# Weights split into high and low parts once and kept in DRAM for the later row groups

## The chip, the cores and the metric

The kernel runs on one core of a Trainium2 chip. The metric is device time in microseconds (us) of one execution, the median of several runs; smaller is better.

## What is computed

One layer of a streaming encoder: 2048 prompt rows and 128 sample rows (8 batches of 16) of width 1024 are normalised, projected to 3072 columns, run through three kinds of attention with gates, projected back to 1024, normalised and added to the input. Cut to what matters here:

```
qa, ka, va, ga, qb, kb, vb, gb, qm, gm = split(rmsnorm(x, g_pre) @ w_in)
oa = band attention of 6 heads (own 64-row chunk and 8 before it, learned bias)
ob = grouped-query window attention of 6 heads (own chunk and 2 before it, ALiBi, sinks)
om = cross-attention of 4 heads into 256 memory tokens
y  = x + rmsnorm(concat(oa*silu(ga), ob*silu(gb), om*silu(gm)) @ w_out, g_post)
```

Everything is float32 and has to come out with nearly that accuracy. Both projections use the same weights for all rows.

## The kernel before

**Precision.** A projection is three passes of matmuls in a reduced-precision type (fp32r): high part times high part, high times low, low times high. So each operand exists as a pair: a rounded high part and the low part that is left over. `project_T` (line 184) multiplies a 128-column weight tile with 512 rows in 24 matmuls (8 blocks of the inner dimension by three passes); `project_N` (line 196) uses two weight tiles for one block of 128 rows, again 24 matmuls.

**Weights.** w_in and w_out lie in DRAM as a list of 128 x 1024 tiles of 512 KB (`wt`; `W_TILES`, line 32). `load_w` (line 131) makes a pair of one: SP (SyncE, which issues most transfers) loads the tile into one of three `wraw` buffers (line 138), ACT copies it rounded into the high half of a `whl` buffer (line 139), and DVE or POOL in turn subtracts the two into the low half (line 140). `whl`, 1 MB each, has three buffers as well. `weights(name)` calls `load_w` at each use, so a tile is loaded and split again in each row group. Four more tiles (`wm`) are for the memory tokens, and one, "last", serves the end of the program alone.

**Rows.** The 2048 rows go in four groups of 512, groups 0 to 3; group 0 takes the 128 sample rows along. Each group projects (24 tiles), attends, and then projects out (8 tiles, "o", in the loop from line 907; in the last group in another form, with two tiles loaded into free parts of the arrays `xn` and `sh`, line 928). Steps of a group stand in a string of `ORDERS` (line 42): M is attention into memory, V, K, Pa and Pb project, Aa and Ab attend, S are the sample rows, X loads keys and values of the group before from DRAM, F finishes the group before (normalise, add x, store), L and N load and scale the next group's rows, Q projects some of the next group's columns.

**Who orders.** The program is written in that order, and a scheduler puts the instructions of each engine in a fixed sequence; an engine then takes its own strictly in order and waits for semaphores. SP is such a queue too: a transfer that waits for its buffer holds up all that stand behind it.

**Names for later.** `psT` and `psN` are the results of the two projections. In attention `sa` are scores, `sba` probabilities (lines 727 to 732: add bias and take the minimum on DVE, exponential on ACT, reciprocal and scaling on DVE), `pt` their transposes, which lines 208 and 209 split on ACT and DVE into `sh`; `oa`, `ob`, `om` (line 260) are the products with the values, merged by lines 267 and 268 into `sums`. `sbm` (line 653) and `sbb` (line 809) are the same for the memory and the window attention. Line 220 copies halves of q, line 891 splits the attention's result for the output projection on POOL.

Of the kernel before, what the change touches and what calls it, by code (L numbers as in the profile page):

```python
# [9 lines left out]
F32 = mybir.dt.float32  # L10
F32R = mybir.dt.float32r
# [20 lines left out]
W_TILES = [("q", 6), ("g", 6), ("q", 7), ("g", 7), ("v", 0, 0), ("v", 0, 1),  # L32
           ("k", 0), ("q", 0), ("g", 0), ("k", 1), ("q", 1), ("g", 1), ("v", 1, 0), ("v", 1, 1),
           ("k", 3), ("q", 3), ("g", 3), ("q", 4), ("g", 4), ("q", 5), ("g", 5), ("k", 2), ("q", 2), ("g", 2)]
W_TILES += [("o", c, r) for c in range(4) for r in range(2)] + [("last",)]

LAST, EARLY = 2, 2
# [8 lines left out]
W_AT = {name: i for i, name in enumerate(W_TILES)}  # L46
# [3 lines left out]
def encoder_step(ctx, tc, x_p, x_s, xT0, xT, mem, memT, wt, wm, g_pre, g_mem, g_post, rel_rev, sink,  # L50
# [3 lines left out]
    pe, act, dve, pool, sp = nc.tensor, nc.scalar, nc.vector, nc.gpsimd, nc.sync  # L54

    cst = ctx.enter_context(tc.tile_pool(name="cst", bufs=1))
    wrawp = ctx.enter_context(tc.tile_pool(name="wrawp", bufs=3))
    whlp = ctx.enter_context(tc.tile_pool(name="whlp", bufs=3))
    xp = ctx.enter_context(tc.tile_pool(name="xp", bufs=2))
    nbp = ctx.enter_context(tc.tile_pool(name="nbp", bufs=2))  # L60
    sbp = ctx.enter_context(tc.tile_pool(name="sbp", bufs=5))
# [7 lines left out]
    drp = ctx.enter_context(tc.tile_pool(name="drp", bufs=1, space=DRAM))  # L69
# [54 lines left out]

    skew_d = drp.tile([6, 128 * 768], F32, name="skew_d")
    e_d = drp.tile([6, 768], F32, name="e_d")
    kctx_d = [drp.tile([128, 2, 512], F32, name=f"kctx{i}") for i in range(6)]
    vctx_d = [drp.tile([128, 4, 256], F32, name=f"vctx{i}") for i in range(6)]


    def load_w(src, hl=None):

        raw = wrawp.tile([128, 1024], F32, tag="wraw", name="wraw")
        if hl is None:
            hl = whlp.tile([128, 2, 1024], F32R, tag="whl", name="whl")
        eng = (dve, pool)[turn["s"] % 2 if turn["s"] > 2 else 0]
        for m in [slice(0, 1024)] if turn["s"] else [slice(0, 512), slice(512, 1024)]:
            sp.dma_start(out=raw[:, m], in_=src[:, m])
            act.activation(hl[:, 0, m], raw[:, m], AF.Copy)  # L139
            eng.tensor_tensor(hl[:, 1, m], raw[:, m], hl[:, 0, m].bitcast(F32), ALU.subtract)  # L140
        turn["s"] += 1
        return hl

    def weights(*name):
        return load_w(wt[W_AT[name]])

    def rms_scale(ss, n, rstd):
        dve.tensor_scalar(rstd[:, :n], ss[:, :n], 1.0 / D, EPS, ALU.mult, ALU.add)
# [338 lines left out]
    def gains():  # L487
        t = xp.tile([128, D], F32, tag="x", name="gpost")
        sp.dma_start(out=t, in_=g_post.partition_broadcast(128))
        return t, stp.tile([128, 32], F32, tag="pst", name="pst", bufs=2)  # L490
# [96 lines left out]
    for g in range(NG):  # L587
# [262 lines left out]
        for step in ORDERS[g].split():  # L850
            what, j = step[:-1], int(step[-1])
# [41 lines left out]
        if g < NG - 1:  # L893
# [13 lines left out]
            for c in range(4):  # L907
                ws = [weights("o", c, r) for r in range(2)]
# [11 lines left out]
        for c in range(EARLY):  # L920
            ws = [weights("o", c, r) for r in range(2)]
# [3 lines left out]
                    act.activation(spare[:, i] if f == LAST else mo[:, i, f], ps[:, 128 * (f % 2):128 * (f % 2) + 128], AF.Copy)  # L925
        room = [t.rearrange("p (a b) -> p a b", a=2) for t in (sh[:, 5376:7424], xn[:, 8192:])]
        wl = weights("last")
        ws = [load_w(wt[W_AT["o", EARLY + j // 2, j % 2]], (room + [None] * 2)[j]) for j in range(4)]
        gpost, st = gains()
        for i in range(4):  # L930
            split_mixed(mixlast, i, LAST, mo[:, i, LAST])
# [2 lines left out]
            o = mo[:, i].rearrange("p a b -> p (a b)")  # L934
# [152 lines left out]
```

## Time and profile before

| | us |
|---|---|
| median of 3 runs (1195.86 to 1201.51) | 1199.81 |
| the profiled execution | 1199.29 |
| its span, first to last instruction | 1197.5 |

Row groups by the profile: group 0's output projection ends at about 414 us, group 1's at about 684 and group 2's at about 955; the first step of the next group (V) follows at once on PE, to about 429, 697 and 967. The profile lists for each engine its busy time, for each group of equal instructions their count, mean duration and the idle time ahead of them with what ended it, and for any stretch of time the busy time of each engine, the granted clock of TensorE (1.00 is full speed), and the busy share and rate of the 16 DMA engines. PE is TensorE's matmuls, PEld its loads of stationary operands, DVE, ACT and POOL are VectorE, ScalarE and GpSimd.

Matmuls are pipelined, and their busy time runs into each other; so a PE that is 100% busy in a stretch is issuing without a pause, and what it can lose shows as idle time or as a lower clock.

### The profile page before, as it was taken

How to read it: one execution, taken by the hardware profiler on the slowest of the kernel's cores; microseconds unless marked ns; L12 is line 12 of the kernel's file. 1: busy time of each engine (PE TensorE's matmuls, PEld its weight loads, DVE VectorE, ACT ScalarE, POOL GpSimd, SP SyncE). 2: the span in 40 equal slices, each digit the busy share in tenths (PEclk: the TensorE clock that was granted, in tenths of full speed). 3: DMA queues.
4: the chain of work that ended last, by engine and by line, in shares of the span. 5: the costliest groups of instructions: out<-in, count | busy, mean ns of one | idle time of the engine just before them, and what ended most of it. 6: DMA issues, size and time to landing. Idle time of an engine off the chain costs nothing.

```text
span 1197.5 us, 20992 instructions
## 1 busy us (share of the span) xinstructions
PE 1137.5 (95%) x7794; PEld 1024.5 (86%) x7794; DVE 840.0 (70%) x1911; ACT 689.5 (58%) x1609; POOL 362.2 (30%) x286
## 2 busy tenths in 40 slices
PE   7899999999989999999999999999988998999897
PEld 6789898897679988898888988898778987988797
DVE  7648666777784457779997336679997336679965
ACT  6546565655544565558664455557765444667652
POOL 5411210211261552122433552122333450221441
PEclk9899999999889999999999999999999998999999
DMA  7673552624621593333311493333321471432213
GB/s 264 211 226 130 172 181 57 232 83 151 240 71 53 176 341 119 110 111 112 126 58 36 133 360 115 111 114 123 115 63 36 129 285 54 126 97 89 90 54 106
DMA packets 62239, 163.43 MB, mean 136 GB/s; under 512 B 8109, under 2 KB 19379, under 8 KB 62137
## 3 DMA queue, kind: packets, MB, share of 16 engines
q1 hardware_dynamic: 58392, 152.66, 38.4%
q0 software_dynamic: 3744, 9.44, 2.7%
q8 instruction: 61, 1.00, 0.3%
q14 instruction: 42, 0.34, 0.1%
HBM read 140.95 MB, written 23.48 MB: 137 GB/s over the span
## 4 chain that ended last, share of the span: by engine, by line
PE 74%; DVE 16%; ACT 3%; issue 3%; DMA 2%; POOL 1%; SPq 0%; DVEq 0%; POOLq 0%; ACTq 0%
PE psT L191 33%; PE psN L202 23%; PE pt L247 5%; PE oa L260 4%; PE sa L241 3%; DVE sh L209 3%; DVE whl L140 1%; DVE sba L727 1%; PE om L260 1%; DVE sbb L798 1%; DVE sbb L809 1%; PE ss L358 1%; PE so L392 1%; PE ob L260 1%; PE sm L241 1%
## 5 line engine op out<-in xcount | busy, mean ns | idle before, releaser
L191 PE MATMUL psT<-xn,whl 128*128 128x512 f32 (+2 forms) x2400 | 531.8, 370 | 11.3 <-ACT whl L139 6.8
L191 PEld LDWEIGHTS psT<-xn,whl 128*128 128x128 f32 x2400 | 410.1, 192 | 73.9 <-ACT whl L139 7.1
L140 POOL TENSOR_TENSOR whl<-wraw,whl 128x1024 fp32r<-128x1024 f32 x64 | 155.7, 2433 | 357.5 <-ACT whl L139 303.7
L202 PE MATMUL psN<-whl,sh 128*128 128x256 f32 x1296 | 162.2, 283 | 1.5 <-POOL sh L891 1.3
L202 PEld LDWEIGHTS psN<-whl,sh 128*128 128x128 f32 x1296 | 156.4, 189 | 3.7 <-POOL sh L891 1.5
L139 ACT ACTIVATE whl<-wraw 128x1024 fp32r<-128x1024 f32 (+1 forms) x132 | 138.2, 1047 | 33.8 <-PE psN L202 13.7
L202 PE MATMUL psN<-whl,xn 128*128 128x256 f32 x1080 | 143.0, 283 | 3.1 <-ACT stgN L618 1.1
L202 PEld LDWEIGHTS psN<-whl,xn 128*128 128x128 f32 x1080 | 133.4, 189 | 7.2 <-issue 1.6
L209 DVE TENSOR_TENSOR sh<-pt,sh 128x512 fp32r<-128x512 f32 (+2 forms) x206 | 123.7, 625 | 21.5 <-ACT sh L208 20.5
L208 ACT ACTIVATE sh<-pt 128x512 fp32r<-128x512 f32 (+2 forms) x206 | 104.4, 547 | 41.0 <-PE pt L247 34.0
L729 ACT ACTIVATE sba<-sba,sta 128x640 f32<-128x640 f32 (+4 forms) x96 | 73.1, 761 | 65.8 <-DVE sta L727 64.0
L140 DVE TENSOR_TENSOR whl<-wraw,whl 128x1024 fp32r<-128x1024 f32 (+1 forms) x68 | 98.9, 1455 | 15.8 <-ACT whl L139 15.4
L631 POOL TENSOR_TENSOR mo<-sums,gr 128x256 f32<-128x256 f32 (+1 forms) x44 | 45.0, 1022 | 186.3 <-DVE sums L268 169.0
L727 DVE CUSTOM_DVE_ANT_0 sba<-sa,nbA 128x640 f32<-128x640 f32 (+4 forms) x96 | 70.6, 735 | 33.2 <-PE sa L241 32.4
L260 PE MATMUL oa<-sh 128*128 128x256 f32 (+1 forms) x504 | 82.0, 285 | 10.9 <-DVE sh L209 7.7
L260 PEld LDWEIGHTS oa<-sh 128*128 128x128 f32 x504 | 71.5, 192 | 17.0 <-DVE sh L209 9.6
L497 DVE TENSOR_TENSOR mo<-psN,gpost 128x256 f32<-128x256 f32 x52 | 22.1, 424 | 73.8 <-ACT junk L496 73.7
L247 PE MATMUL pt<-ident,sba 128*128 128x128 f32 x420 | 67.5, 281 | 3.4 <-DVE sba L732 3.2
L800 ACT ACTIVATE sbb<-sbb,stb 128x256 f32<-128x256 f32 (+1 forms) x96 | 47.3, 493 | 27.7 <-DVE stb L798 27.5
L732 DVE TENSOR_SCALAR sba<-sba,sta 128x640 f32<-128x640 f32 (+4 forms) x96 | 59.9, 624 | 2.6
L496 ACT ACTIVATE junk<-psN 128x256 bf16<-128x256 f32 x52 | 20.0, 384 | 62.3 <-PE psN L202 62.2
L247 PEld LDWEIGHTS pt<-ident,sba 128*128 128x128 f32 x420 | 49.6, 143 | 7.1 <-DVE sba L732 4.2
(282 smaller groups left out, 1643.9 us busy)
## 6 DMA issues: line engine op xcount, KB each, us to landing
wraw<-in_wt SPq DMA_DIRECT2D x128, 512.0 KB, 3.6
xr<-in_x_p SPq DMA_DIRECT2D x16, 512.0 KB, 5.8
nbA<-skew_d SPq DMA_DIRECT2D x24, 320.0 KB, 3.2
vta<-in_cva SPq DMA_DIRECT2D x12, 512.0 KB, 4.5
xt<-in_x_p SPq DMA_DIRECT2D x12, 512.0 KB, 5.0
out_y_p<-mo SPq DMA_DIRECT2D x12, 512.0 KB, 4.7
vctx<-sh SPq DMA_DIRECT2D x9, 512.0 KB, 5.4
kctx<-sh SPq DMA_DIRECT2D x9, 512.0 KB, 4.1
```

Of the source, the lines that this page charges most:

```text
L139: act.activation(hl[:, 0, m], raw[:, m], AF.Copy)
L140: eng.tensor_tensor(hl[:, 1, m], raw[:, m], hl[:, 0, m].bitcast(F32), ALU.subtract)
L191: pe.matmul(ps[:, :n], w[:, a, k * 128:(k + 1) * 128], src[:, b, k, c0:c0 + n], start=(i == 0), stop=(i == 23))
L202: pe.matmul(ps[:, :256], stat(a, k), w[:, b, (k % 4) * 256:(k % 4 + 1) * 256], start=(k == ks[0] and i == 0), stop=(k == ks[-1] and i == 2))
L208: act.activation(hi, src, AF.Copy)
L209: eng.tensor_tensor(lo, src, hi.bitcast(F32), ALU.subtract)
L241: pe.matmul(out[:, c:c + n], q[:, part, qc:qc + 128], kt[:, h, kc:kc + n], start=part == h, stop=part != h)
L247: pe.transpose(pt[:, i * 128:(i + 1) * 128], b, ident)
L260: pe.matmul(o[:, oc:oc + w], v, pt[:, part, c:c + w], start=(first and i == 0), stop=(i == n - 1), skip_group_check=True)
L727: dve.tensor_tensor_reduce(sb[:, :nk], s[:, c0:c0 + nk], nb[h][:, 640 - nk:], 1.0, 3.0e38, ALU.add, ALU.min, st[:, e:e + 1])
L729: act.activation(sb[:, :nk], sb[:, :nk], AF.Exp, bias=st[:, e:e + 1], scale=-1.0, accum_out=st[:, 2 + e:3 + e])
L732: dve.tensor_scalar(sb[:, :nk], sb[:, :nk], st[:, 4 + e:5 + e], 0.5, ALU.mult, ALU.mult)
```

## The change

In `weights`, the first use of a tile (always in group 0, but for "last") splits it as before and then stores the pair, 1 MB, to a new DRAM tensor `whl_d`. Each later use loads the pair from there straight into a `whl` buffer: one transfer of 1 MB, without `wraw`, ACT, DVE or POOL. `whl` gets a fourth buffer. At the end, the four output tiles take the same path, two of them into the free parts of `xn` and `sh`. The tiles for the memory tokens and "last" stay as they were.

```
-    whlp = ctx.enter_context(tc.tile_pool(name="whlp", bufs=3))
+    whlp = ctx.enter_context(tc.tile_pool(name="whlp", bufs=4))
...
+    whl_d = drp.tile([len(W_TILES), 128, 2048], F32, name="whl_d")
...
+    kept = set()
...
-    def weights(*name):
-        return load_w(wt[W_AT[name]])
+    def weights(*name, hl=None):
+
+        n = W_AT[name]
+        if n in kept:
+            if hl is None:
+                hl = whlp.tile([128, 2, 1024], F32R, tag="whl", name="whl")
+            sp.dma_start(out=hl.bitcast(F32), in_=whl_d[n].rearrange("p (a b) -> p a b", a=2))
+            return hl
+        hl = load_w(wt[n], hl)
+        if name[0] != "last":
+            kept.add(n)
+            sp.dma_start(out=whl_d[n].rearrange("p (a b) -> p a b", a=2), in_=hl.bitcast(F32))
+        return hl
...
-        ws = [load_w(wt[W_AT["o", EARLY + j // 2, j % 2]], (room + [None] * 2)[j]) for j in range(4)]
+        ws = [weights("o", EARLY + j // 2, j % 2, hl=(room + [None] * 2)[j]) for j in range(4)]
```

The scheduler orders everything anew. Three places follow; line numbers below 125 are the same in both kernels, those of the changed one then run up to 14 higher (138 becomes 141, 706 becomes 720). In the whole program SP's order has 32 stores of pairs (L158) and 96 loads of them (L153, of which one goes to `xn` and one to `sh`), and 37 split loads are left.

SP in group 0, about a third into it, in the projections of the first two head pairs, before (`vta`, `mo<-in_ckaT` and `kctx` are sample caches and kept keys):

```order
L138 DMA wraw<-in_wt 128x1024 x2
L696 DMA vta<-in_cva 128x1024
L597 DMA out_akTs<-ksm 128x128
L667 DMA kctx_124<-sh 256x1x512
L696 DMA vta<-in_cva 128x1024
L138 DMA wraw<-in_wt 128x1024 x3
L407 DMA mo<-in_ckaT 128x4x256 x2
L597 DMA out_akTs<-ksm 128x128
```

The same place now:

```order
L611 DMA out_akTs<-ksm 128x128
L158 DMA whl_d<-whl 128x2048
L141 DMA wraw<-in_wt 128x1024
L681 DMA kctx_125<-sh 256x1x512
L710 DMA vta<-in_cva 128x1024
L158 DMA whl_d<-whl 128x2048
L141 DMA wraw<-in_wt 128x1024
L158 DMA whl_d<-whl 128x2048
L141 DMA wraw<-in_wt 128x1024
L421 DMA mo<-in_ckaT 128x4x256 x2
L611 DMA out_akTs<-ksm 128x128
```

Ahead of nearly each load of a raw tile there is now the store of the pair made some tiles earlier.

SP where group 2 begins, before (`out_y_p` and `xr` belong to the finishing of group 1, `xt` to the scales of group 3, `vctx` and `kctx` keep this group's values and keys):

```order
L138 DMA wraw<-in_wt 128x1024 x2
L512 DMA out_y_p<-mo 128x1024
L509 DMA xr<-in_x_p 128x1024
L512 DMA out_y_p<-mo 128x1024
L157 DMA xt<-in_x_p 128x1024
L668 DMA vctx_130<-sh 128x1024
L138 DMA wraw<-in_wt 128x1024 x2
L668 DMA vctx_131<-sh 128x1024
L512 DMA out_y_p<-mo 128x1024
L157 DMA xt<-in_x_p 128x1024 x2
```

And now:

```order
L523 DMA xr<-in_x_p 128x1024
L153 DMA whl<-whl_d 128x2048 x2
L682 DMA vctx_131<-sh 128x1024
L682 DMA vctx_132<-sh 128x1024
L526 DMA out_y_p<-mo 128x1024
L171 DMA xt<-in_x_p 128x1024
L153 DMA whl<-whl_d 128x2048
L526 DMA out_y_p<-mo 128x1024
L171 DMA xt<-in_x_p 128x1024
L681 DMA kctx_125<-sh 256x1x512
L153 DMA whl<-whl_d 128x2048 x2
```

The transfers around the weights are the same and in nearly the same order; each weight tile is now 1 MB in place of 512 KB, and it waits for a `whl` buffer rather than a `wraw` buffer.

POOL where group 3 begins, before (L511 adds x to the finished rows, L149 is a power for the scales, L840 and L841 load kept keys and values):

```order
L140 TENSOR_TENSOR whl<-wraw,whl 128x1024
L841 DMA sh<-vctx_131 128x1024
L149 TENSOR_TENSOR fin<-fin,expo 128x1
L511 TENSOR_TENSOR mo<-mo,xr 128x1024 x2
L140 TENSOR_TENSOR whl<-wraw,whl 128x1024
L511 TENSOR_TENSOR mo<-mo,xr 128x1024
L140 TENSOR_TENSOR whl<-wraw,whl 128x1024 x3
L840 DMA sh<-kctx_125 128x2x512
```

And now:

```order
L855 DMA sh<-vctx_131 128x1024
L163 TENSOR_TENSOR fin<-fin,expo 128x1
L855 DMA sh<-vctx_132 128x1024
L163 TENSOR_TENSOR fin<-fin,expo 128x1
L525 TENSOR_TENSOR mo<-mo,xr 128x1024 x3
L721 MEMSET nbA 64x64
L722 MEMSET nbA 64x64
L854 DMA sh<-kctx_126 128x2x512
```

The subtractions of the splits are gone from POOL's sequence; nothing else takes their place.

## The prediction, made before the changed kernel ran

> **What bounds the kernel now.** I read the busy times first, then stretches of time, then the waits of PE.
>
> ```profile
> PE 1137.5 (95%) x7794; PEld 1024.5 (86%) x7794; DVE 840.0 (70%) x1911; ACT 689.5 (58%) x1609; POOL 362.2 (30%) x286
> ```
>
> PE is busy 95% of the span, so taking work from ACT, DVE and POOL can at most win PE's idle time and the time it runs at a lower clock. Where that is, the stretches show (columns: stretch, its length, busy us and count by engine, granted clock, DMA share, GB/s).
>
> ```profile
> core 0: us, PE busy (x) PEld busy (x) DVE busy (x) ACT busy (x) POOL busy (x), PEclk, DMA share, GB/s
> 697.00:760.00 63.00, 63.00 (x312) 52.62 (x311) 39.10 (x73) 36.58 (x65) 17.96 (x11) 1.00 0.60 211
> 430.00:1142.00 712.00, 684.77 (x4323) 610.66 (x4321) 521.14 (x1145) 426.92 (x953) 227.15 (x178) 0.99 0.38 124
> 550.00:643.00 93.00, 86.32 (x537) 76.44 (x536) 88.38 (x195) 63.69 (x158) 33.00 (x30) 0.96 0.28 86
> 810.00:910.00 100.00, 91.48 (x564) 79.53 (x562) 94.59 (x218) 69.57 (x174) 32.01 (x30) 0.98 0.29 90
> 1080.00:1142.00 62.00, 57.12 (x350) 49.54 (x348) 58.06 (x152) 44.47 (x106) 24.18 (x24) 0.97 0.26 79
> 995.00:1010.00 15.00, 11.47 (x45) 9.07 (x44) 9.93 (x19) 6.87 (x13) 2.36 (x1) 0.77 0.21 68
> ```
>
> In most of a group PE never pauses (697 to 760: 63 of 63 us). From 430 to 1142 it idles 712 - 684.8 = 27.2 us, and 20.1 of these lie in the three stretches that end in the attention of a group: 6.7 + 8.5 + 4.9. There DVE is busy 95%, 94% and 94%. The rest is mostly one place near 1000. **So groups 1 to 3 are PE-bound for the most part and DVE-bound at their ends**, and the change can win only there.
>
> ```profile
> PE oa L260 <- DVE sh L209: 7.7, 9, 2.7
> PE psT L191 <- ACT whl L139: 6.8, 2, 5.7
> PE pt L247 <- DVE sbm L653: 4.3, 4, 1.5
> PE psT L191 <- DVE whl L140: 0.5, 1, 0.5
> ```
>
> PE's longest waits in total (us, times, longest) are for DVE's work in attention. For a weight's split it waits 6.8 us, 5.7 of it in a single wait at the program's start, where the split remains.
>
> **What is removed, and what it is worth.** 96 of 133 splits go.
>
> ```profile
> L140 POOL TENSOR_TENSOR whl<-wraw,whl 128x1024 fp32r<-128x1024 f32 x64 | 155.7, 2433 | 357.5 <-ACT whl L139 303.7 <-issue 30.8 <-DMA vtm<-in_cvm 17.6
> L139 ACT ACTIVATE whl<-wraw 128x1024 fp32r<-128x1024 f32 (+1 forms) x132 | 138.2, 1047 | 33.8 <-PE psN L202 13.7 <-DMA wraw<-in_wt 10.1 <-PE psT L191 8.3
> L140 DVE TENSOR_TENSOR whl<-wraw,whl 128x1024 fp32r<-128x1024 f32 (+1 forms) x68 | 98.9, 1455 | 15.8 <-ACT whl L139 15.4
> ```
>
> That frees ACT of 96 x 1.05 = 101 us, DVE of about 48 x 1.46 = 70 and POOL of 48 x 2.43 = 117. Little of it stands in PE's way: it lies under matmuls. What counts is DVE's share in the three ends:
>
> ```profile
> 550.00:643.00 93.00, 4.87 (x4) 7.56 (x3) 0.96 0.28 86
> 810.00:910.00 100.00, 6.85 (x5) 9.72 (x4) 0.98 0.29 90
> 1080.00:1142.00 62.00, 4.00 (x3) 7.23 (x3) 0.97 0.26 79
> ```
>
> (line 140 alone: DVE, then POOL). DVE loses 4.87 + 6.85 + 4.00 = 15.7 us of work. POOL's part counts too, since some DVE instructions stand still while POOL subtracts:
>
> ```profile
> 1000.04 2.36 POOL L140 TENSOR_TENSOR whl<-wraw,whl 128x1024 fp32r<-128x1024 f32 x1 [11.55 <-ACT whl L139]
> 1000.30 0.85 PE L241 MATMUL sa<-sh,xn 128*128 128x320 f32 x4 [1.87 <-DVE sta L727]
> 1000.35 2.40 DVE L732 TENSOR_SCALAR sba<-sba,sta 128x640 f32<-128x640 f32 x1
> 1002.81 1.75 PE L247 MATMUL pt<-ident,sba 128*128 128x128 f32 x7 [1.66 <-DVE sba L732]
> 1004.56 6.54 PE psT L191 x21
> ...
> 601.52 1.77 DVE L732 TENSOR_SCALAR sba<-sba,sta 128x640 f32<-128x640 f32 x1
> 833.41 2.56 DVE L220 CAST xn<-xn 64x512 fp32r<-64x512 f32 x1
> 871.12 2.26 DVE L220 CAST qr<-qr 64x512 fp32r<-64x512 f32 x1
> L732 DVE TENSOR_SCALAR sba<-sba,sta x96: 280/553/2399, 146.4 to 1147.8; 128x640 f32<-128x640 f32 x72, 128x128 f32<-128x128 f32 x6, 128x256 f32<-128x256 f32 x6, 128x384 f32<-128x384 f32 x6
> L220 DVE CAST xn<-xn x8: 420/421/2556, 331.4 to 1066.8; 64x512 fp32r<-64x512 f32 x8
> ```
>
> A scaling that takes 0.55 us in the median took 2.40 and ended with POOL's subtraction (1000.04 + 2.36 = 1002.40); a cast of 0.42 took 2.56. In the three ends I find such stretches by POOL's line 140 in three instructions, those at 601.5 (1.77 for 0.55), 833.4 and 871.1 (2.26 for 0.42): 1.2 + 2.1 + 1.8 = 5.1 us. So DVE gets 15.7 + 5.1 = 20.8 us free where it bounds; PE's idle time there, 20.1, caps the gain. I take two thirds of 20.8, **-13.9**: the waits for line 653 (4.3 us) have POOL's line 891 beside them, which stays, and the waits of line 260 end a chain over PE, ACT and DVE that a free DVE shortens but does not remove. The bounds are 0 (only the chain counts) and 20.1.
>
> Near 1000 us the wait of 1.66 goes, and most of the slow clock behind it: 21 matmuls took 6.54 us where 72 of the same kind take 16.80 elsewhere (0.233 each), 6.54 - 21 x 0.233 = 1.6 us. **-3.3.** The other idle time there, 1.87 us, waits for line 727, whose queue on DVE holds no split; it stays.
>
> **What is added in group 0.** 32 stores of 1.05 MB, each behind the split that also frees the raw buffer for the load behind it in SP's order, so SP waits no longer than before. The cost is DMA time: the 16 engines move some 370 GB/s when full (rows below), so 2.8 us a store, 90 us in all over 414, where they are now about half busy.
>
> ```profile
> 0.00:430.00 430.00, 403.70 (x3071) 365.63 (x3072) 286.72 (x695) 242.43 (x599) 123.64 (x97) 0.97 0.50 164
> 5.00:20.00 15.00, 11.94 (x51) 10.43 (x51) 13.12 (x9) 11.20 (x15) 11.89 (x7) 1.00 0.98 367
> 430.00:450.00 20.00, 20.00 (x93) 16.43 (x92) 11.19 (x19) 12.57 (x21) 11.75 (x7) 1.00 1.02 373
> 685.00:715.00 30.00, 29.14 (x174) 25.51 (x173) 11.60 (x20) 16.71 (x30) 16.30 (x8) 1.00 1.01 366
> 955.00:980.00 25.00, 23.80 (x149) 20.96 (x148) 8.53 (x16) 12.48 (x25) 16.26 (x8) 1.00 0.99 351
> ```
>
> The place that can feel it is the start, full from 5 to 20 us with PE idle 3 of 15; four stores fall into the first 40 us. One of them on the path: **+3**. Bounds 0 and four, 11.
>
> **What is added in groups 1 to 3.** Each load is 0.52 MB larger. Where a group turns into the next, the DMA engines are full already (the last three rows). With the splits that start there as a count of the tiles (3, 6 and 5; the same stretches, line 139 alone),
>
> ```profile
> 430.00:450.00 20.00, 3.15 (x3) 1.00 1.02 373
> 685.00:715.00 30.00, 6.01 (x6) 1.00 1.01 366
> 955.00:980.00 25.00, 4.99 (x5) 1.00 0.99 351
> ```
>
> the queue grows by 1.57 MB / 373 = 4.2 us, 3.15 / 366 = 8.6 and 2.62 / 351 = 7.5: 20.3 in all, the upper bound. Against it stand the buffers: with four `whl`, three tiles lie ahead of the one in use, and a tile feeds 24 matmuls.
>
> ```profile
> 696.92 16.80 PE psT L191 x72
> DMA to landing us min/median/max: 3.3/3.7/8.2
> ```
>
> Three tiles last 16.8 us. A raw tile lands 8.2 us after its issue at worst; the larger one takes 1.4 more (0.52 MB at 373), 9.6, and with the grown queue 13.8, 18.2 and 17.1. The second and third are late by 1.4 and 0.3: **+2**. Behind a load that waits for its `whl` buffer SP holds the row loads and score biases; before, the load waited for `wraw` at the same places. Elsewhere the engines are 38% busy on average and the loads are hidden. At the program's end, the four loads in place of splits fall into 0.25 of DMA share and cost nothing.
>
> **Sum.** 1199.3 (the profiled execution, half a microsecond under the median of 1199.8) - 13.9 - 3.3 + 3 + 2 = **1187 us**. 0.5%, about what a measurement of this kernel can tell from no change, is 6 us.
>
> **Rivals.**
>
> *The weights come late at the turns of groups (slower).* If the three tiles ahead do not cover the loads, because the stores and row loads in the same queue grow with them, PE waits out the full 20.3 us, and the clock falls after each wait. That it does so is shown at the start:
>
> ```profile
> PE psT L191 <- DVE cs L535: 5.3, 1, 5.3
> 50.00:55.00 5.00, 3.85 (x18) 3.85 (x19) 4.09 (x10) 1.89 (x3) 0.29 (x2) 0.50 0.60 181
> ```
>
> after 5.3 us without a matmul the next 5 run at 0.50. Three turns at 1.6 us, as near 1000, make 4.8. Then 1199.3 - 17.2 + 3 + 20.3 + 4.8 = 1210. It decides from the point at which a pair takes over 16.8 us to land. For it speaks the DMA share of 1.0 at all three turns, against it the worst landing of 8.2 us today.
>
> The Trainium skill ("TensorE: Matmul & The Clock Gate", Part 1) says that the clock halves after an idle window of about 3.4 us and returns only after as long a busy one. The row agrees (5.3 us idle, then 0.50). By that rule, waits under 3.4 us cost no clock, and this rival without its clock term would be 1205; near 1000, though, two idles of 1.87 and 1.66 us were followed by the slow clock, so I keep it.
>
> *The ends of groups are bound by the chain, not by DVE's throughput (no change).* Then only the place near 1000 is won and the added transfers stay: 1199.3 - 3.3 + 5 = 1201. For it: the waits of PE name many lines, and line 140 on DVE for 0.5 us in all.
>
> *All idle time goes (larger gain).* PE pauses nowhere from 430 to 1142 and group 0 hides its stores: 1199.3 - 27.2 = 1172.
>
> That the change does not do what it says can be left aside: the order of the program has its 32 stores and 96 loads.
>
> **How the numbers follow.** Forecast 0.50 (its own range 1179 to 1194: half and all of the gain at the ends, 0 to 6 us of cost), larger gain 0.15, no change 0.19, late weights 0.16. Faster by over 0.5% is 0.50 + 0.15 = 0.65, within 0.5% 0.19, slower 0.16. The range reaches to the larger gain and to the late weights with three more for a second store on the path in group 0: 1170 to 1213.
>
> **What would show it.** Right: DVE's line 140 has some 21 instructions and POOL's 17; in the ends of groups 1 to 3 DVE's busy share falls below 90% and PE's idle time from 20 us to some 6; scalings of line 732 no longer take over 1.5 us there. Wrong: PE waits named for a transfer of `whl`; a clock of 0.5 at the turns; PE's idle time in the first 100 us larger by more than 5 us; or ends of groups that keep their idle time with DVE under 90%, which would mean the chain.

## The result: slower by 0.9%

| | us |
|---|---|
| before, median of 4 runs (1195.86 to 1201.51) | 1199.45 |
| changed, median of 4 runs (1207.95 to 1210.96) | 1209.50 |
| ratio, 95% interval | 1.0087, 1.0058 to 1.0115 |
| span of the profiled execution, before and changed | 1197.5, 1206.8 |

The forecast was 1187. The time lies inside the range (1170 to 1213), the sign is wrong. First the busy times of the changed kernel, and three rows of its transfers (KB of each, median us from issue to landing):

```profile
PE 1141.7 (95%) x7794; PEld 1025.2 (85%) x7794; DVE 750.6 (62%) x1863; ACT 597.2 (49%) x1513; POOL 240.7 (20%) x238
...
whl<-whl_d SPq DMA_DIRECT2D x94, 1024.0 KB, 5.1
whl_d<-whl SPq DMA_DIRECT2D x32, 1024.0 KB, 5.9
wraw<-in_wt SPq DMA_DIRECT2D x32, 512.0 KB, 7.5
```

(Line numbers of the changed kernel are 3 higher than before's at the split, L143 for L140, and 14 higher behind it, L205 for L191.) The change does what it says: DVE is rid of 89 us, ACT of 92, POOL of 121. A raw tile, though, now lands 7.5 us after its issue; nearly all of these loads lie in group 0. Before, the row for the first 400 us (over the whole program it is 3.6) was:

```profile
wraw<-in_wt SPq DMA_DIRECT2D x37, 512.0 KB, 4.3
```

To see where the time went, I cut each trace at the same work: from the start to the 1,728th matmul of the projections (psT and psN counted together), then to the 2,880th, the 3,840th and the end. The cuts lie in the output projections of groups 0, 1 and 2, so the four stretches are called group 0 to group 3 from here on. Before, and then the changed kernel (columns as in the prediction):

```profile
0.00:395.60 395.60, 369.30 (x2783) 331.52 (x2784) 270.35 (x659) 220.52 (x556) 101.85 (x81) 0.97 0.48 158
395.60:679.00 283.40, 276.72 (x1826) 251.26 (x1824) 207.80 (x441) 170.95 (x382) 97.70 (x74) 0.99 0.40 129
679.00:937.30 258.30, 247.36 (x1582) 220.66 (x1581) 190.59 (x416) 156.41 (x349) 83.02 (x64) 0.99 0.40 132
937.30:1191.00 253.70, 244.08 (x1609) 221.10 (x1608) 169.39 (x392) 141.10 (x320) 79.06 (x66) 0.98 0.36 117
```

```profile
0.00:415.50 415.50, 379.36 (x2782) 336.83 (x2783) 269.12 (x657) 217.09 (x553) 100.07 (x80) 0.95 0.67 238
415.50:694.30 278.80, 273.77 (x1827) 248.45 (x1826) 175.82 (x425) 139.14 (x349) 54.85 (x58) 1.00 0.56 197
694.30:948.60 254.30, 246.00 (x1582) 219.91 (x1581) 161.62 (x399) 127.28 (x319) 44.73 (x48) 1.00 0.54 195
948.60:1200.30 251.70, 242.54 (x1610) 220.02 (x1608) 142.09 (x378) 113.17 (x291) 40.52 (x51) 0.99 0.49 173
```

PE does the same number of matmuls in each stretch (give or take one). **Group 0 is 19.9 us longer; groups 1 to 3 are 4.6, 4.0 and 2.0 shorter.** So the change wins 10.6 us where it was to win, and loses nearly twice that in group 0, where the stores, a fourth buffer and some early loads of pairs were added. Of the 19.9 us, 9.8 are idle time of PE (36.1 against 26.3) and the rest is busy time at a lower clock.

Most of it is lost in one place, the end of group 0's attention: the 1,250th matmul of the projections ends at 279.3 us before and at 283.4 now, the 1,400th at 354.4 and 374.7. Three pieces of 10 us there, before and then changed:

```profile
340.00:350.00 10.00, 10.00 (x47) 8.27 (x47) 8.88 (x14) 4.86 (x12) 7.46 (x4) 0.88 0.04 14
350.00:360.00 10.00, 10.00 (x73) 9.34 (x72) 6.28 (x10) 3.95 (x12) 3.33 (x2) 1.00 0.35 105
360.00:370.00 10.00, 10.00 (x87) 10.00 (x86) 4.28 (x11) 5.21 (x18) 1.24 (x1) 1.00 0.01 2
```

```profile
340.00:350.00 10.00, 4.05 (x19) 3.15 (x19) 9.84 (x11) 5.29 (x10) 8.94 (x8) 0.67 0.14 46
350.00:360.00 10.00, 10.00 (x49) 8.81 (x49) 5.67 (x13) 3.32 (x12) 2.00 (x2) 0.82 0.84 305
360.00:370.00 10.00, 5.75 (x22) 4.61 (x21) 9.72 (x11) 5.03 (x14) 5.98 (x4) 0.70 0.47 159
```

And its last wait there, on PE's timeline (start, busy us, in brackets the idle time ahead and what ended it):

```profile
360.08 1.20 PE L255 MATMUL sm<-mK,xn 128*128 128x256 f32 x8
365.52 8.19 PE L205 MATMUL psT<-xn,whl 128*128 128x512 f32 x24 [4.25 <-DVE qr L233]
```

The 24 matmuls of a Q tile wait 4.25 us for DVE, which stands in the attention's tail, and then take 8.19 us: the clock has dropped. In the order of before, two such rows of 24 stood at this place and kept PE at work while DVE went through the tail:

```profile
336.77 1.76 PE L260 MATMUL oa<-sh 128*128 128x256 f32 x7 [2.70 <-DVE sh L209]
338.32 7.70 PE L191 MATMUL psT<-xn,whl 128*128 128x512 f32 x24
345.87 1.03 PE L247 MATMUL pt<-ident,sbm 128*128 128x128 f32 x8
346.65 1.19 PE L241 MATMUL sm<-mK,xn 128*128 128x256 f32 x8
347.69 5.77 PE L191 MATMUL psT<-xn,whl 128*128 128x512 f32 x24
```

On the clock, the Trainium skill ("TensorE: Matmul & The Clock Gate", Part 1) has the clock halve after an idle window of about 3.4 us. The changed kernel's row, slow after 4.25 us of idle time, agrees. In the rows of before, though, the first 24 matmuls took 7.70 us, 1.93 more than the next 24, behind an idle time of only 2.70 us and two shorter ones just ahead of it (1.02 and 0.71): in this kernel waits of under 3.4 us were followed by a slow clock too.

### The profile page after: what moved, and what is told of

It is laid out like the page before. It is cut to its first block, busy times and chain, and to the rows that moved or that the text cites. A ratio compares the mean times of both kernels' runs of the same rounds, so it can differ in the third digit from the quotient of the medians.

```text
span 1206.8 us, 20781 instructions
## 1 busy us (share of the span) xinstructions
PE 1141.7 (95%) x7794; PEld 1025.2 (85%) x7794; DVE 750.6 (62%) x1863; ACT 597.2 (49%) x1513; POOL 240.7 (20%) x238
## 4 chain that ended last, share of the span: by engine, by line
PE 77%; DVE 10%; DMA 6%; ACT 2%; issue 2%; SPq 1%; POOL 1%; DVEq 0%; POOLq 0%; ACTq 0%
PE psT L205 36%; PE psN L216 21%; PE pt L261 5%; PE oa L274 4%; PE sa L255 3%; DMA wraw<-in_wt 2%; PE ob L274 2%; DVE sh L223 1%; DVE sba L741 1%; PE om L274 1%; PE ss L372 1%; DMA xk<-in_xT 1%; DVE sba L746 1%; DMA whl_d<-whl 1%; PE so L406 1%
## 5 line engine op out<-in xcount | busy, mean ns | idle before, releaser
L205 PE MATMUL psT<-xn,whl 128*128 128x512 f32 (+2 forms) x2400 | 529.4, 370 | 18.7 <-ACT whl L142 5.8
L205 PEld LDWEIGHTS psT<-xn,whl 128*128 128x128 f32 x2400 | 412.3, 192 | 82.3 <-issue 6.6
L511 DVE TENSOR_TENSOR mo<-psN,gpost 128x256 f32<-128x256 f32 x52 | 22.0, 422 | 84.9 <-ACT junk L510 84.8
L143 POOL TENSOR_TENSOR whl<-wraw,whl 128x1024 fp32r<-128x1024 f32 x17 | 42.3, 2487 | 125.7 <-ACT whl L142 111.7
L261 PE MATMUL pt<-ident,sba 128*128 128x128 f32 x420 | 64.9, 276 | 2.3 <-DVE sba L746 2.2
L510 ACT ACTIVATE junk<-psN 128x256 bf16<-128x256 f32 x52 | 19.9, 382 | 76.1 <-PE psN L216 75.8
L255 PE MATMUL sa<-sh,qr 128*128 128x320 f32 (+4 forms) x240 | 51.5, 324 | 4.1 <-DVE sta L741 3.9
L746 DVE TENSOR_SCALAR sba<-sba,sta 128x640 f32<-128x640 f32 (+4 forms) x96 | 52.4, 547 | 2.7
L142 ACT ACTIVATE whl<-wraw 128x1024 fp32r<-128x1024 f32 (+1 forms) x38 | 38.9, 1032 | 25.1 <-DMA wraw<-in_wt 14.9
```

The costliest lines, as they stand in the source:

```text
L205: pe.matmul(ps[:, :n], w[:, a, k * 128:(k + 1) * 128], src[:, b, k, c0:c0 + n], start=(i == 0), stop=(i == 23))
L255: pe.matmul(out[:, c:c + n], q[:, part, qc:qc + 128], kt[:, h, kc:kc + n], start=part == h, stop=part != h)
L261: pe.transpose(pt[:, i * 128:(i + 1) * 128], b, ident)
L746: dve.tensor_scalar(sb[:, :nk], sb[:, :nk], st[:, 4 + e:5 + e], 0.5, ALU.mult, ALU.mult)
```

## The experiments

In the table, group 0 is the first stretch above, groups 1 to 3 the other three added up, each from the one profiled execution of that kernel; times and ratios are from all runs, each ratio against the kernel before on the same chip.

| kernel | us | ratio, 95% interval | group 0 | groups 1 to 3 |
|---|---|---|---|---|
| before | 1197.8 to 1200.0 | | 395.6 | 795.4 |
| changed | 1209.5 | 1.0087 [1.0058, 1.0115] | 415.5 | 784.8 |
| e1_q_again | 1206.7 | 1.0085 [1.0056, 1.0114] | 417.1 | 781.4 |
| e2_stores_only | 1225.5 | 1.0237 [1.0218, 1.0256] | 413.2 | 802.6 |
| e3_no_stores | 1202.3 | 1.0037 [1.0021, 1.0053] | 408.4 | 787.4 |
| e4_four_buffers | 1217.1 | 1.0165 [1.0146, 1.0185] | 403.7 | 804.5 |
| e5_three_buffers | 1205.4 | 1.0044 [1.0024, 1.0065] | 404.0 | 791.8 |
| e6_one_held | 1206.6 | 1.0055 [1.0034, 1.0077] | 405.8 | 790.5 |
| e7_three_no_stores | 1199.1 | 1.0010 [0.9994, 1.0025] | 395.1 | 795.1 |
| e8_three_act_queue | 1223.1 | 1.0192 [1.0163, 1.0221] | 420.0 | 797.5 |
| e9_small_stores | 1195.6 | 0.9966 [0.9947, 0.9986] | 395.6 | 792.3 |
| e10_three_pool_queue | 1222.0 | 1.0184 [1.0146, 1.0223] | 413.2 | 801.4 |
| e12_held_pool_queue | 1218.8 | 1.0157 [1.0120, 1.0195] | 420.6 | 791.3 |
| e13_keep_qgk | 1202.8 | 1.0022 [1.0003, 1.0042] | 404.0 | 793.5 |
| e14_keep_qgk_later | 1214.3 | 1.0122 [1.0092, 1.0153] | 411.2 | 792.5 |
| e16_keep_vo | 1211.7 | 1.0097 [1.0066, 1.0128] | 393.9 | 806.3 |
| e15_keep_qgk_held | 1222.1 | 1.0188 [1.0155, 1.0220] | 406.5 | 804.0 |
| e17_rows_four | 1236.2 | 1.0311 [1.0288, 1.0334] | 416.4 | 813.0 |
| e18_rows_four_no_stores | 1215.1 | 1.0128 [1.0111, 1.0146] | 398.6 | 808.5 |
| e19_rows_three | 1253.7 | 1.0447 [1.0421, 1.0472] | 418.6 | 822.3 |

### The parts alone

My first theory, T1, was a queue that stands still: in the changed kernel's order, four loads of pairs for the next group's Q tiles stand on SP ahead of the last sample attention's loads. T2 and T3 are in the expectations.

**e1_q_again**: those four are split again.

```
-                new_qg.append((*block_q(g + 1, 6 + j), block_g(g + 1, 6 + j)))
+                again = [load_w(wt[W_AT[k, 6 + j]]) for k in 'qg'] if g == 0 else [None] * 2
+                new_qg.append((*block_q(g + 1, 6 + j, again[0]), block_g(g + 1, 6 + j, again[1])))
```

> Three theories of the loss in group 0, which is 20 us there (the trace of the changed kernel against that of before, by the time at which as many projection matmuls were done) against 11 us won in groups 1 to 3. T1, order of the queue: in group 0 the direct loads of the next group's four Q tiles (q and g, 6 and 7) stand on SP ahead of the loads of the last sample attention, each waits for a whl buffer, and the four pairs then hold all four buffers until they are used some 80 us later. T2, traffic: the 32 stores of 1.05 MB delay the other transfers of group 0. T3: the fourth whl buffer alone, through the order that the scheduler then chooses. Here the four Q tiles of the Q step in group 0 are split again from the raw weights in place of being loaded. T1: group 0 loses 5 us or less and the kernel takes some 1196 us. T2: 1207 to 1210, as the changed kernel. T3: as the changed kernel.

1206.7, and group 0 at 417.1. T1, which had 1196, falls: the early loads are not the cause.

**e2_stores_only**: stores and four buffers, but every tile is split at each use.

```
         if n in kept:
+            return load_w(wt[n], hl)
```

> Four whl buffers and the 32 stores in group 0, but every tile is split from the raw weights in every group as before; the kept pairs are never loaded. T1 (order of the queue): no direct load stands in the way, so 1200 to 1203. T2 (traffic of the stores): the 20 us of group 0 stay and nothing is won later, 1215 to 1220. T3 (fourth buffer): as T2 in the first group, without a forecast for the rest.

1225.5, worse than any theory gave. Group 0 stays long without one pair loaded (413.2), and groups 1 to 3 are 7.2 us longer than before although they issue the same transfers as before.

**e3_no_stores**: only the first pair is stored, and all loads read it.

```
-            sp.dma_start(out=hl.bitcast(F32), in_=whl_d[n].rearrange("p (a b) -> p a b", a=2))
+            sp.dma_start(out=hl.bitcast(F32), in_=whl_d[stored[0]].rearrange("p (a b) -> p a b", a=2))
...
+            if not kept:
+                stored.append(n)
+                sp.dma_start(out=whl_d[n].rearrange("p (a b) -> p a b", a=2), in_=hl.bitcast(F32))
             kept.add(n)
-            sp.dma_start(out=whl_d[n].rearrange("p (a b) -> p a b", a=2), in_=hl.bitcast(F32))
```

> The changed kernel with the store of the first tile alone; all direct loads read that one pair. It leaves out 31 of the 32 stores, so its later groups compute with the first tile's weights; the work and the loads are as many and as large as in the changed kernel. T1 (order of the queue): the four early direct loads stay, so 1205 to 1209. T2 (traffic of the stores): group 0 is as fast as before and the 11 us of the later groups are won, 1188 to 1190. T3: as the changed kernel, 1207 to 1210.

1202.3, in none of the three ranges: the stores are worth 7.2 us of time, 7.1 of them in group 0 (415.5 against 408.4). That leaves group 0 at 12.8 us over before without them, so T2 explains less than half.

**e4_four_buffers**: the kernel before with a fourth buffer.

```
-    whlp = ctx.enter_context(tc.tile_pool(name="whlp", bufs=3))
+    whlp = ctx.enter_context(tc.tile_pool(name="whlp", bufs=4))
```

> The kernel before with four whl buffers in place of three and nothing else. T1 and T2: within 2 us of the kernel before, 1198 to 1201. T3 (the buffer and the order that the scheduler chooses with it): moved by 5 us or more, to slower if it is to explain the loss.

**One more buffer and nothing else costs 19.3 us** (1217.1 against 1197.8); in the profiled executions it is 8.1 in group 0 and 9.1 after it. Its stretch at the same place, and its wait there:

```profile
350.00:360.00 10.00, 6.61 (x16) 5.20 (x17) 9.87 (x11) 2.98 (x10) 5.86 (x3) 0.66 0.16 52
```

```profile
353.39 8.64 PE L191 MATMUL psT<-xn,whl 128*128 128x512 f32 x24 [4.25 <-DVE qr L219]
```

It is the wait of the changed kernel, 4.25 us for `qr` and the slow clock behind it. The transfers are those of before, which points to the order: the scheduler, which knows that a buffer is free, places the rows of all engines anew. That it is the order and not the buffer is shown only with the order held fixed, below.

### Three buffers

**e5_three_buffers** is the changed kernel with `bufs=3` for `whlp`.

> The changed kernel with three whl buffers, as before, in place of four. The first four runs give three prices: the fourth buffer alone +19.3 us (1217.1 against 1197.8), the stores +8.4 on top of it (1225.5), the direct loads -16.0 (1209.5 for the whole change against 1225.5). T3 (the fourth buffer costs, through the order in which the scheduler then puts the matmuls): if the prices add up, 1190, faster than before by 0.6%. T4 (the direct loads gain only because a fourth buffer lets them run ahead): 1200 to 1206, as weights come late at the turns of groups. T1 (early loads of the Q tiles block SP): they are still there, so the loss of group 0 stays, 1205 to 1209.

1205.4, in T4's range and also in that of T1, which e1 had already refuted; T3's 1190 is missed by 15 us. Group 0 is 11.5 us shorter than with four (404.0 against 415.5) and groups 1 to 3 are 7.0 longer. There PE now waits for pairs (engine, matmul and who ended the wait: us in total, times, longest):

```profile
PE psN L216 <- DMA whl<-whl_d: 5.6, 6, 1.5
```

**e6_one_held**: four buffers, one of them taken until the end of group 0.

```
+    held = whlp.tile([128, 2, 1024], F32R, tag="whl", name="held")
+    dve.tensor_copy(held[:, 0, :8], ones[:, :8])
     bctx = None
...
+        if g == 0:
+            dve.tensor_tensor(free, held[:, 0, :8].bitcast(F32), mo[:, 0, :, 0], ALU.mult)
```

> The changed kernel with four whl buffers, one of which is taken ahead of group 0 by a tile that is read only when the mixed features of group 0 are all there: three buffers in group 0, four from then on. T3: of the 20 us that group 0 loses, the part beyond the stores (12.6 us in the run without stores) goes: 1196 to 1200. T1: 1205 to 1209. If the fourth buffer costs in the later groups too, it stays above the kernel with three buffers throughout by 5 to 10 us; if four are needed there, it is faster than that one.

1206.6, outside T3's 1196 to 1200. About half of group 0's loss goes (405.8, so 9.7 of 19.9 us, where T3 had 12.6), and with it most of what the fourth buffer wins later (790.5, where three buffers throughout take 791.8 and four 784.8).

**e7_three_no_stores**: e3 with three buffers.

> The run with the first store alone (31 of 32 stores left out, all direct loads read one pair) with three whl buffers: the price of the stores with three buffers. With four it was 7.2 us (1209.5 against 1202.3). T3: 1183 to 1186, and the predicted gain of 15 us in groups 1 to 3 is there. T2 in a weaker form, that stores cost only where the order already leaves PE short: equal to the three-buffer kernel with stores within 3 us.

1199.1, no different from before, where T3 had 1183 to 1186. The stores' price is 6.3 us here, more than the 3 of T2's weaker form. Group 0 is as long as before (395.1), and so are groups 1 to 3: with three buffers, the loads of pairs win little over the splits (nothing here, 3.6 us in e5, 3.1 in e9).

**e8_three_act_queue**: e5, with `act.dma_start` for the store.

> Three whl buffers, and the stores are issued by ACT in place of SP. If the stores cost because they stand in SP's queue and hold back the loads behind them: faster than the kernel with three buffers by 4 us or more. If they cost by the traffic: the same within 3 us. If ACT's own queue is held up by them: slower.

1223.1, slower by 17.7 us than with the stores on SP's queue, as the third case had it. How long ACT stood still for a store, its trace does not tell.

### What a store costs by

**e9_small_stores**: e7, with the other 31 stores at 64 KB.

```
+            else:
+                sp.dma_start(out=whl_d[n][:, :128], in_=hl[:, 0, :128].bitcast(F32))
```

> Three whl buffers, the first store whole and the other 31 at their places in SP's order, each with 64 KB of its 1 MB (and all direct loads read the first pair, so the later groups compute with the first tile's weights; it leaves out 15 of 16 parts of the stored bytes). Without those stores the kernel takes 1199.1, with them whole 1205.4. Traffic (the bytes of the stores slow the other transfers of group 0): 1198 to 1201. Queue (a store waits at the head of SP's queue for the low part of its split, 104 us in all, and holds back the loads behind it): 1203 to 1206.

1195.6, 2.4 us under the range for traffic and far from that for the queue, and group 0 at 395.6. The raw tiles land in 3.9 us here, as in e3 and e7 (3.8 and 4.0), and in 7.3 in e5, so the bytes are what slows their landing. It is no clean proof for the time, since the order of PE's rows differs from e5 too.

**e10_three_pool_queue** is e5 with `pool.dma_start` for the store, **e12_held_pool_queue** the same on e6.

> Three whl buffers, whole stores, issued by POOL in place of SP. On ACT's queue they cost 17.7 us more than on SP's, PE's idle time in group 0 rose from 25.4 to 39.5 us. Traffic: 1203 to 1207, as on SP's queue. Queue of SP: 1199 to 1202. An issuing engine that stands still for the split of another engine (as ACT did): over 1210, since POOL also does half of the splits and the scalings of the mixed rows.

> Four whl buffers with one held through group 0, and the stores on POOL's queue. With the stores on SP's queue this kernel takes 1206.6. Traffic: 1205 to 1208. Queue of SP: 1200 to 1203. POOL standing still: over 1212.

1222.0 and 1218.8, both as the last case had it. In e10 POOL stands still at its stores, 48.5 us in eleven waits for a low part that DVE makes:

```profile
POOL whl_d L158 <- DVE whl L143: 48.5, 11, 11.7
```

That is not the whole of it: of e10's 18.8 us over e5 in the table, 9.6 lie in groups 1 to 3, where no pair is stored, so not all of it is the stores' own (in e8, 16.0 us lie in group 0 and 5.7 behind it).

### Fewer tiles

If loads win at the ends of groups and lose at the turns, one should keep only the tiles of the ends. Three buffers; `if name[0] != "last"` becomes `if name[0] in "qgk"` (**e13_keep_qgk**), the same with `and name[1] < 6` (**e14_keep_qgk_later**), or `in "vo"` (**e16_keep_vo**); **e15_keep_qgk_held** is e14's line in e6.

> Three whl buffers; only the 20 tiles of q, g and k are kept and loaded as pairs, the 12 of v and o are split again in every group. 20 stores in place of 32; at the turns of groups, where o and v are loaded and the DMA engines are full, a tile is 0.5 MB as before. Theory A (the stores' bytes cost by number, and the pairs of o and v come late at the turns): stores 6.3 x 20/32 = 4 us in place of 6.3, the waits for pairs (5.6 us with all tiles kept) gone, the gain at the ends kept: 1193 to 1198. Theory B (what is gained is gained on o and v too, by the free ACT, DVE and POOL at the turns): 1203 to 1208.

> As the last, without the four Q tiles (q and g, 6 and 7), whose stores fall into the first 40 us: 16 tiles kept. These four stores are a third of the loss of group 0 by the times at which as many projection matmuls were done (3.5 of 8.8 us stand by 66 us). Theory A with the start as the place: 2 to 3 us less than with 20 tiles, 1190 to 1195. If the Q step at the ends of groups is where the gain lies: 2 to 4 us more than with 20 tiles.

> The complement: three whl buffers, only the 12 tiles of v and o are kept. Theory A: the cost of 12 stores (2 us) and the late pairs at the turns, and no gain at the ends: 1203 to 1208. Theory B: 1193 to 1199.

> The 16 tiles kept, four whl buffers of which one is held through group 0. Groups 1 to 3 with all tiles kept took 784.5 us with four buffers and 791.6 with three, the splits of before with four buffers 804.3. Theory A, if the fourth buffer helped only the pairs of o and v: 2 us or more above the three-buffer kernel with the same tiles. If it helps the pairs everywhere: 3 to 6 us below it.

1202.8, 1214.3, 1211.7, 1222.1. The first three lie outside theory A's ranges, and e13 alone at the edge of B's; e15 is 7.8 us above e14, on A's side (2 us or more). Above all, group 0 came out at 404.0, 411.2 and 393.9 us with 20, 16 and 12 stores: **it does not go by the number of stores**. Prices taken from kernels that each have an order of their own do not add up. So the last three kernels take the order away.

### The order held fixed

**e17_rows_four** is the changed kernel, **e18_rows_four_no_stores** is e3 and **e19_rows_three** is e5, each in the order of before. A table holds, for each engine, the instructions of before by the number in which they were written down, row by row as the scheduler had placed them; each instruction that still exists is chained behind the one ahead of it:

```
+    for e, rows in ROWS.items():
+        last = None
+        for row in rows.split():
+            k, n = (row.split("+") + ["1"])[:2]
+            for j in range(int(k), int(k) + int(n)):
+                i = at.get((e, j))
...
+                if last is not None:
+                    tc.add_manual_dep(i, last.name, mybir.DependencyInfo(
+                        mybir.DependencyClass.NoSync, mybir.DependencyReason.DATA), reason="rows")
+                last = i
```

PE, DVE, ACT and POOL then run the rows of before, less the splits that are gone; SP's transfers are placed by the scheduler. Line numbers in these kernels are some 220 to 232 higher than in the changed one (L437 is its L205).

> In every kernel so far the scheduler chose the order of the rows on each engine anew: of before's 7523 rows on PE some 1300 to 2000 stand elsewhere. Here the whole change, with four whl buffers, runs in the order of before: PE, DVE, ACT and POOL are chained row by row as they stood there (splits that are gone left out), and only the transfers that SP issues are placed by the scheduler. Theory O (the new order is what the change loses by): faster than before by 0.5% or more, 1186 to 1194, group 0 within 6 us of before. Theory S (the stores' bytes and the loads themselves cost what was measured): group 0 stays 7 to 10 us longer and the kernel takes 1200 to 1206.

> The same, in the order of before, with the first store alone; all direct loads read that pair, so the later groups compute with the first tile's weights, and 31 of 32 stores are left out. The difference to the run with stores is the price of their bytes at a fixed order. Theory O: within 3 us of it. Theory S: 6 to 8 us less. The predicted gain of groups 1 to 3 (15 us) at a fixed order would give 1183 to 1186; a gain bound by the chain of the attention (idle time at the ends of groups 20 to 14 us) 1190 to 1195.

> The whole change with three whl buffers in the order of before. With a free order three buffers were 4 us faster than four (1205.4 against 1209.5). Theory O: with the order fixed a buffer more cannot cost, so this one is slower than the run with four by 2 to 8 us, by late pairs at the turns of groups. Theory of a cost of the buffer itself: faster than it by 3 us or more.

1236.2, 1215.1 and 1253.7. Both theories' times are missed. Theory O, that the new order is what the change loses by, falls as a whole: in the order of before the change is 26.7 us slower than in its own. With three buffers the loss against four has the sign that theory O gave, but 17.5 us in place of 2 to 8. But the parts can now be read one by one.

*The fourth buffer.* At a fixed order it wins 17.5 us (1253.7 against 1236.2), and in group 0 2.2 (418.6 against 416.4): PE waits 23.1 us for pairs in e19, and in e17 no wait of PE is for one. So what it costs in group 0 with a free order, 8.1 (e4 against before), 11.5 (changed against e5) and 13.3 us (e3 against e7), comes from the order chosen with it. The same shows without stores and with four buffers: group 0 takes 398.6 in the order of before and 408.4 in the order chosen.

*The stores.* 21.1 us (1236.2 against 1215.1), 17.8 of them in group 0. The largest piece is one wait of PE there in e17:

```profile
59.51 1.92 PE L445 MATMUL psN<-whl,sh 128*128 128x256 f32 x14
73.65 4.64 PE L445 MATMUL psN<-whl,sh 128*128 128x256 f32 x20 [12.23 <-POOL whl L365]
```

The DMA engines were 0.58 busy from 60 to 74, so this one is not the bytes but a raw tile's load that leaves SP late: SP issued such loads at 54.32, 64.16 and 73.63, in e18 at 50.92, 55.17, 58.65 and 61.30. With a free order the stores cost 7.1 to 9.5 us in group 0 (changed against e3, e5 against e7, e2 against e4).

*The ends of groups.* The same rows of PE at the three ends, before and then e18:

```profile
556.40:667.90 111.50, 104.82 (x699) 95.29 (x698) 95.44 (x200) 71.33 (x176) 39.12 (x32) 0.97 0.26 80
822.30:925.90 103.60, 94.45 (x625) 84.30 (x624) 93.55 (x198) 69.42 (x171) 34.21 (x30) 0.98 0.26 83
1065.30:1145.60 80.30, 75.42 (x465) 66.01 (x464) 74.13 (x191) 56.45 (x136) 27.45 (x26) 0.98 0.28 87
```

```profile
567.60:676.80 109.20, 103.97 (x701) 95.13 (x699) 85.31 (x194) 61.05 (x165) 25.80 (x27) 0.97 0.38 135
842.70:941.70 99.00, 92.45 (x624) 83.10 (x623) 82.64 (x191) 60.37 (x159) 24.91 (x26) 1.00 0.37 131
1083.00:1161.70 78.70, 75.17 (x465) 65.96 (x463) 66.57 (x187) 47.84 (x127) 17.19 (x22) 0.98 0.43 153
```

DVE gets 28.6 us free (10.1 + 10.9 + 7.6), and the stretches become 2.3 + 4.6 + 1.6 = 8.5 us shorter. PE still idles 15.3 of 20.7 us, with DVE at 78, 83 and 85% where it was 86, 90 and 92.

*The turns of groups.* The stretches that follow each turn, again the same rows, before and then e18:

```profile
407.10:468.40 61.30, 61.30 (x380) 54.58 (x378) 34.53 (x66) 37.88 (x68) 31.58 (x18) 1.00 0.74 262
691.00:766.50 75.50, 75.47 (x401) 64.40 (x402) 42.20 (x81) 40.76 (x73) 25.19 (x16) 1.00 0.59 210
948.70:1017.50 68.80, 64.07 (x369) 55.76 (x368) 34.00 (x68) 35.02 (x65) 26.21 (x15) 0.95 0.52 178
```

```profile
410.10:479.60 69.50, 63.91 (x380) 56.47 (x378) 26.67 (x62) 29.55 (x60) 17.62 (x13) 0.95 0.83 304
700.30:786.90 86.60, 77.69 (x401) 65.81 (x402) 33.03 (x76) 30.50 (x62) 10.38 (x10) 0.94 0.73 265
964.60:1035.30 70.70, 64.60 (x368) 56.39 (x368) 24.93 (x63) 25.59 (x55) 13.02 (x10) 0.95 0.67 242
```

8.2 + 11.1 + 1.9 = **21.2 us lost at the turns.** The longest wait there is 8.9 us, from 717.4 to 726.3. The profile names nothing that ended it; the semaphores and the other engines' rows do. The pair that PE needs had landed at 714.4. What PE waits for is DVE, which waits for ACT, which stands in its fixed order at the scaling of a row of the next group (`xt`) until that row has landed:

```profile
722.50 1.06 ACT L404 ACTIVATE xt<-xt 128x1024 f32<-128x1024 f32 x1 [15.37 <-DMA xt<-in_x_p]
724.16 0.68 DVE L473 TENSOR_TENSOR sh<-psT,sh 64x512 fp32r<-64x512 f32 x1 [16.71 <-ACT sh L472]
726.29 7.82 PE L437 MATMUL psT<-xn,whl 128*128 128x512 f32 x24 [8.91 <-issue]
```

That row was 12.3 us under way, where before the slowest of twelve took 8.3, and the DMA engines were full at 415 GB/s:

```profile
717.00:726.00 9.00, 0.38 (x2) 0.00 (x0) 1.18 (x2) 2.73 (x5) 0.00 (x0) 0.69 1.02 415
```

The wait of 5.6 us at the first turn ends with an output: POOL stands 9.5 us until the store of the sample rows (`out_y_s`) has landed, and ACT, DVE and PE follow. Both waits stand in e17 too, 9.5 us each. How much of such a delay is the transfer's later issue and how much the larger pairs in the same engines was not separated. The changed kernel, in its own order, between the same counts of projection matmuls:

```profile
426.80:490.10 63.30, 63.30 (x397) 56.61 (x396) 29.20 (x67) 32.18 (x64) 17.34 (x14) 1.00 0.92 337
705.60:781.00 75.40, 75.40 (x403) 64.33 (x402) 32.61 (x74) 29.90 (x63) 8.87 (x10) 1.00 0.82 308
959.90:1027.40 67.50, 62.24 (x351) 53.88 (x349) 22.88 (x58) 24.44 (x52) 12.35 (x9) 0.95 0.69 256
```

206.2 us against 205.6 before, and no idle time at the first two turns. In this order ACT scales the row of the second turn only at 728.9, behind its copies of the projections' results, and in the whole program it stands 4.8 us for such rows (36.0 in e18).

## Why the prediction was wrong

**The step that failed is "What is added in group 0", +3.** Group 0 cost 19.9 us. Two things are in it:

- The stores, 7.1 to 9.5 us with a free order. Here the mechanism was one of those named (the DMA engines' time), and the size lay inside its bounds, 0 and 11; one store on the path was too few. "SP waits no longer than before" was wrong as well: in the piece of e17 shown loads leave SP later, and the raw tiles of group 0 land later, 7.5 us after issue for 4.3.
- The order, 8.1 to 13.3 us, for which the sum had no term at all. The prediction took the fourth buffer as a gain only and read durations off the order of before. In the new order PE has too few matmuls left for the tail of group 0's attention, waits, and runs on at a clock of 0.67 to 0.82 in the rows shown. That the order costs group 0 its time was shown (e17 against e19, where the buffer alone wins; e3 against e18). Which of the moved rows does it was not tried.

**Ends of groups, -13.9: right in kind, too large.** At a fixed order it is -8.5. Two thirds of DVE's freed time were taken to reach PE; it was 8.5 of 28.6 us. The wrong sign named in advance came true, ends that keep their idle time (three quarters of it) with DVE under 90%. That speaks for the rival that the chain over the engines bounds them for the larger part; no run changed the chain itself. In the changed kernel the three ends show it too (before, PE idled 20.1 us in them, now 13.6, where some 6 were to be left):

```profile
556.00:650.00 94.00, 90.46 (x570) 79.28 (x570) 83.53 (x219) 60.73 (x162) 20.27 (x24) 1.00 0.45 152
821.00:918.00 97.00, 90.57 (x563) 78.85 (x562) 82.00 (x204) 60.38 (x161) 19.54 (x25) 1.00 0.42 142
1084.00:1150.00 66.00, 62.36 (x394) 54.50 (x392) 57.02 (x167) 40.24 (x110) 16.16 (x21) 1.00 0.46 158
```

**Near 1000 us, -3.3: the cause went, the gain did not come.** No scaling stands still behind POOL any more (longest 1.27 us, from 2.40), and the wait of 1.66 us is gone. Yet the stretch from 948.7 is only 1.3 us shorter, and 1.9 longer at a fixed order. Two things are in the way. The slow clock stayed: the other wait, 1.88 us for line 741 (727 before), is still there, and behind it 20 matmuls take 6.46 us where 21 took 6.54. And a new wait of 3.39 us came ahead of it (3.09 in e18). It ends with a copy of ACT that had stood for the landing of an output (`out_av`), so here too another transfer came late, not a pair.

```profile
979.98 0.38 ACT L632 ACTIVATE stgN<-psN 128x256 f32<-128x256 f32 x1 [2.00 <-DMA out_av<-stgN]
980.42 18.61 PE L205 MATMUL psT<-xn,whl 128*128 128x512 f32 x72 [3.39 <-ACT stgN L632]
1015.84 6.46 PE L205 MATMUL psT<-xn,whl 128*128 128x512 f32 x20
```

```profile
L746 DVE TENSOR_SCALAR sba<-sba,sta x96: 268/553/1271, 150.5 to 1159.3; 128x640 f32<-128x640 f32 x72, 128x128 f32<-128x128 f32 x6, 128x256 f32<-128x256 f32 x6, 128x384 f32<-128x384 f32 x6
```

**Turns of groups, +2: the size is right for the changed kernel (206.2 against 205.6), the reason is not.** With four buffers the three tiles ahead do cover the loads: neither in the changed kernel nor in e17 or e18 does a wait of PE end with a pair. With three buffers pairs do come late, 6.8 us in e5. What came late beside the larger loads is the rows and outputs in the same queue, which the prediction set aside ("before, the load waited for `wraw` at the same places"): at a fixed order the turns lose 21.2 us, in waits for them and by the slower clock behind these (0.95 and 0.94). That this is close to the 20.3 that the rival "weights come late" put there is luck, and so is the rival's total, 1210, which is met by a sum of other terms.

**Signs and readings.** Of the signs named in advance, DVE's 21 and POOL's 17 subtractions, DVE under 90% at the ends and no scaling over 1.5 us came true, PE's idle time of some 6 us at the ends did not. Of the wrong ones only the last did: no wait of PE for a pair, a clock of 1.00 at the first two turns, and no more idle time in the first 100 us (14.0 against 14.8). Three readings were loose without moving the sum: the scaling of 2.40 us ended 0.35 us after POOL's subtraction (1002.75 and 1002.40), the place near 1000 held 3.5 of the 7.1 us of idle time left, about half and not most, and the forecast's own range of 1179 to 1194 does not come out of its words (half and all of 13.9, with 0 to 6 us of cost, give 1182 to 1195).

Together: 19.9 - 10.6 = +9.3, against a forecast of -12.2. Of the miss of 21.5 us, 16.9 are group 0 and the rest is the smaller gain of groups 1 to 3 (15.2 forecast, 10.6 measured).

No run gave a kernel that computes the same and beats the one before. The nearest are e13 (1202.8) and e5 (1205.4); e9, whose stores move almost no bytes, won 0.3%. Whether a better order for the changed transfers exists is open.

## What to carry to other kernels

Where a scheduler sets the order, an edit's price has two terms, the work it moves and the order that it brings about; one more buffer alone moved this kernel by 19 us. Chaining the rows of the old kernel in the new one separates the two, but the old order is not neutral: here it let ACT stand at rows that now land late. Prices taken from kernels with different orders did not add up. Before trading engine time for traffic, ask which transfers share the DMA engines and who stands for them in order: this change freed 300 us on three engines, little of which stood in PE's way, and paid with 84 MB more traffic (247.3 against 163.4), beside which the raw tiles of group 0 (7.5 us to land for 4.3) and the rows `xt` (7.4 for 5.0 in the median) came later.

## What the runs showed of the hardware

With full engines, transfers moved more than the 370 GB/s on which the prediction reckoned: 415 from 717 to 726 us in e18. The Trainium skill ("Perfetto Trace Analysis", Roofline) gives the 16 DMA engines about 435 GB/s together; no stretch quoted here is above that.

The same 32 stores, issued by ACT or POOL in place of SP, went with some 17 us more (1223.1 and 1222.0 against 1205.4). For POOL the trace shows a part of the cause, the 48.5 us for which it stood at stores that waited for DVE's half. That ACT stood in the same way is argued, not shown, and the time lost in groups 1 to 3, where nothing is stored, is not the stores' own.
